# Value loops of a hybrid decoder block: unit words refilled by halves, first key quarters loaded early, second key input turned in other tiles

## The chip, the cores and the metric

The kernel runs on one core of a Trainium2 chip. The metric is device time in microseconds, the median of several runs. Engines are named as in the profile: PE (TensorE matmuls), PEld (its weight loads), DVE (VectorE), ACT (ScalarE), POOL (GpSimd), SP (SyncE, which here only issues DMAs).

## What is computed

One decoder block over 512 tokens of 2048 channels: RMSNorm, one wide input projection, two groups of attention heads side by side, each gated by a SiLU path, an output projection, a residual and a final RMSNorm. Cut to the parts near the change:

```python
h = _rmsnorm(x, norm_g[l])
proj = h @ w_in[l]
(qa, kca, vca, ksa, vsa, kwa, vwa, za, ga, qb, kb, vb, zb) = jnp.split(proj, offsets, axis=-1)
qa = _rope(_heads(qa, 8, 128))...
kc = _compress(_rope(_heads(kca, 2, 128)), cmp_k_pos[l], cmp_k_w1[l], cmp_k_w2[l])
vc = _compress(_heads(vca, 2, 128), cmp_v_pos[l], cmp_v_w1[l], cmp_v_w2[l])
o_cmp, p_cmp = _compressed_attention(qa, kc, vc)
o_sel = _selected_attention(qa, _rope(ksa), vsa, _select_blocks(p_cmp, S))
o_win = _banded_attention(qa, _rope(kwa), vwa, 512)
y_a = (gates . (o_cmp, o_sel, o_win)) * silu(za)
...
def _compress(kv, pos_emb, w1, w2):      # 31 blocks of 32 tokens, 16 apart, of each of 2 key heads
    flat = blocks of kv + pos_emb        # (B, 31, 2, 32 * 128)
    return silu(flat @ w1) @ w2          # w1: 4096 x 256
```

## The kernel before, in words

All matmuls work on fp32 inputs split into two words, hi (rounded, by ACT) and lo (the rest, by DVE: input minus hi); a product is three matmuls, L110 (hi by hi), L111 and L112 (hi by lo). A weight tile of 128x1024 (512 KB) is loaded by SP into one of the raw buffers (raw0, raw1, raw2, for keys and heads also raw3), split by ACT and DVE into the words whi and wlo (a pool of three buffers for each), and used by PE.

Three parts of the kernel matter here; they follow attention B, whose last part still runs beside the first rows below.

*Last projections and value loops.* Two projections kc, the compressed keys' inputs, lie in pj banks; `turned` (L769) applies the rope to each on DVE (products by L115 to L117 into t1 and t2, sum by L772) and writes kvt0. Then `proj(wz[18])` and `proj(wz[19])` (48 matmuls of 512 columns each) give the compressed values' inputs, which `values` (L763) scales into kvt1. Loop 1 runs over four chunks of the weights wv1: `tok_chunk` (48 matmuls of 256 columns) takes a chunk's words, and after each chunk two compress units of the keys (`compress_unit`, L653), each with two cw halves of 256 KB, split by L511/L512 into words, and 8 matmuls (L674, L675). `build(6)` and `build(7)` (L393 on) form words of x for the later products, also on ACT and DVE (L401 to L407). Loop 2 runs over eight chunks of wv0 (24 matmuls of 280 columns) with one compress unit of the values each. In loop 2, two loads for the keys are issued: a quarter at u = 3, and at u = 4 the sum of two quarters, the first loaded by SP, the second added on top by an accumulating DMA of POOL (`sums`, L739 to L741).

*Keys and heads.* Each of `keys(1)`, `keys(0)`, `pair(0)` (the first head's query and gate) and the later pairs runs `seven` (L538): seven products of 24 matmuls instead of eight, over four weight quarters x1, x2, x3, x4 (q3, q0, q1, q2 of the source) and sums of them. The products are named "22", "p", "21", "12", "u", "w", "q"; between them DVE and ACT form words and sums and run hooks. With `extra` a sum is formed by the DMAs: x4 gets q3 added by POOL (L567), and `extra()` returns the sum of q0 and q2 (for keys `fifth_sum`, for the first head `sum_of_head`, L830), which is split for "12". The key words of group 1 are written to DRAM by POOL in four transfers (`key_words`, L733, Kd<-k), those of group 0 go to KH and KL.

*Order.* Each engine does its instructions in its own order, which the scheduler of the framework sets from when the inputs and buffers come free; `tc.issue_after(x)` puts an instruction behind x in it. A DMA issued by SP or POOL waits for its buffer at the head of that engine's queue, with the later ones behind it.

Of the kernel before, what the change touches and what calls it, by code (L numbers as in the profile page):

```python
# [34 lines left out]
def hybrid_block(ctx, tc, xT, xtm, w0, wv0, wv1, wz, wq, wo0, wos, cw1, cw2, cpos, e2, rope, tabs, sinks, gT, fg, out):  # L35
# [430 lines left out]

    kvstack = xstack.enter_context(ExitStack())
    kv = kvstack.enter_context(sb("kvA", side="right"))
    KH = kv.tile([P, CMP + 1056], F32R, name="KH")[:, 0:CMP + 1024]
    KL = kv.tile([P, CMP + 1056], F32R, name="KL")[:, 0:CMP + 1024]  # L470
    VH, VL = [kv.tile([P, NQ - 1, 2, P], F32R, name=f"V{e}") for e in "HL"]
    VF = kv.tile([P, 2, 2, 256], F32, name="VF")
    VC = [kv.tile([P, P], F32R, name=f"VC{g}") for g in range(2)]
    pps = ExitStack()
    pp = pps.enter_context(sb("pp"))

# [173 lines left out]

        return qq, silu if h == 7 else silu()

    def compress_unit(b, u, acc):  # L653
        F = wk.tile([P, 4, P], F32R, name="F", tag=("ph", "pl")[u % 2])
        hi, lo = [F[:, :, e * 64:e * 64 + 64].rearrange("p j (g b) -> p j g b", g=2) for e in range(2)]
        off, j0 = u // 4, 4 * u % 16
        for g in range(2):
            src = kvts[b][:, g, j0:j0 + 4, off:off + 31]
            act.activation(hi[:, :, g, 0:31], src, AF.Copy)
            dve.tensor_tensor(out=lo[:, :, g, 0:31], in0=src, in1=hi[:, :, g, 0:31].bitcast(F32), op=ALU.subtract)  # L660
        for e, word in enumerate((hi, lo)):
            src = posw[:, b, 4 * u:4 * u + 4, e].unsqueeze(2).to_broadcast([P, 4, 2])
            dve.tensor_copy(word[:, :, :, 31], src)
        wh, wl = words(EVEN)
        for half in range(2):
            n = half if u % 2 else 2
            r = wk.tile([P, S], F32, name="cw", tag="st") if n == 2 else \
                wk.tile([P, S], F32, name="cw", tag=("qh", "ql")[n], bufs=1)
            last["dma"] = nc.sync.dma_start(r, cw1[:, b, u, half * S:half * S + S]).ins
            cs = slice(half * S, half * S + S)  # L670
            split(wh[:, cs], wl[:, cs], r)
        for j in range(4):
            cs = slice(j * 256, j * 256 + 256)
            pe.matmul(acc[:, 0:256], F[:, j], wh[:, cs], start=u == 0 and j == 0, stop=False)  # L674
            pe.matmul(acc[:, 0:256], F[:, j], wl[:, cs], start=False, stop=u == 7 and j == 3)  # L675
# [16 lines left out]
    def compressed_keys(acc):  # L692
# [3 lines left out]
            pe.matmul(kcp[:, 0:64], cw2s[:, 0, i, :], sl[:, i, :], start=i == 0, stop=i == 1)  # L696
        kct = pp.tile([P, 64], F32, name="kct")
        act.activation(kct, kcp[:, 0:64], AF.Copy, scale=0.5)
        k1 = pp.tile([P, 2, CMP], F32R, name="k1w")
        for g, (h, l) in enumerate(((KH[:, 0:CMP], KL[:, 0:CMP]), (k1[:, 0], k1[:, 1]))):  # L700
            src = kct[:, g * 32:g * 32 + 32]
            act.activation(h, src, AF.Copy)
            dve.tensor_tensor(out=l, in0=src, in1=h.bitcast(F32), op=ALU.subtract)
        for e in range(2):
            pool.dma_start(Kd[e, :, 0:CMP], k1[:, e].bitcast(F32))

    def compressed_values(sl):
        for g in range(2):
# [57 lines left out]
    def units(b, us):  # L766
        return [lambda u=u: compress_unit(b, u, cacc[b]) for u in us]

    def turned(ps, out):  # L769
        t1, t2 = rope_mul(wk.tile([P, S], F32, name="t1", tag="t1", bufs=1), wk.tile([P, S], F32, name="t2", tag="t2", bufs=1),  # L770
                          ps, cosA, sinA)
        dve.tensor_tensor(out=out, in0=by_block(t1), in1=by_block(t2), op=ALU.add)  # L772

    banks6 = [bank(e) for e in range(6)]
    vacc = [banks6[0:4], [banks6[4 + t // 2][:, t % 2 * 256:t % 2 * 256 + 256] for t in range(NQ)]]
    first_words = load_unit(wv1[:, 0], 1024, place=MOVING)
    for g in range(2):
        turned(kc[g], kvts[0][:, g, :, 0:32])
    for g in range(2):
        values(proj(wz[18 + g]), g)  # L780
    cacc = [psp.tile([P, S], F32, name="pj", tag="pj"), None]
    early, ready = [], []
    xr = rows(6)
    for u in range(4):
        tok_chunk(wv1, 4, 256, vacc[1], u, True, None if u else first_words)
        for n in (2 * u, 2 * u + 1):
            compress_unit(0, n, cacc[0])
        if u == 0:
            build(6, xr)
            xr = rows(7)  # L790
# [2 lines left out]
    for u in range(8):  # L793
# [4 lines left out]
            cacc[1] = bank(4)  # L798
        compress_unit(1, u, cacc[1])
        if u == 1:  # L800
            compressed_keys(csum)
        if u == 3:
            early.append(load_quarter(wq[0], tags[0], 3))
        if u == 4:
            ready.append(fifth(0))
            sums(*ready, wq[0], 0, 2)

    def gate_evac():
        for t in range(NQ):
# [3 lines left out]
        gc = gates[:, 0, :].rearrange("p (h b) -> p h b", b=3)[:, :, 0]  # L813
        dve.tensor_scalar(gc, gc, rowvalid, None, op0=ALU.mult)

    early += [load_quarter(wq[0], c, quarter) for c, quarter in zip(tags[1:], (0, 2, 1))]
    with tc.issue_after(last["lo"]):
        for ms in (slice(0, 4), slice(4, 8)):
            for e in range(2):
                pool.dma_start(even[e][:, ms], wd[e, :, ms])  # L820
            if not added:
# [607 lines left out]
```

## Time and profile before

| | |
|---|---|
| median of 3 runs | 816.33 us (812.87 to 817.54) |
| profiled execution | 813.13 us, span 811.4 us |
| PE busy | 794.7 us, 98% of the span |
| DVE busy | 689.7 us, 85% |
| ACT busy | 499.6 us, 62% |
| POOL busy | 91.9 us, 11% |
| DMA | 123.17 MB, mean 152 GB/s |

The span is the profiled execution from its first to its last instruction. Stages, by the trace: the two last projections and loop 1 from about 278 to 323 us, loop 2 to 357, keys(1) to 378, keys(0) to 399, pair(0) to 418, then the other heads, attention A and the output projection.

### The profile page before, as it was taken

The numbers are of one execution on the slowest core, as the hardware profiler recorded it, in microseconds if no ns is written. First come the engines' busy times: TensorE is split into PE (matmuls) and PEld (weight loads), VectorE is DVE, ScalarE is ACT, GpSimd is POOL, SyncE is SP. The second block draws the span as 40 slices with busy tenths as digits, with TensorE's granted clock in tenths as the row PEclk, the third lists the DMA queues.
The fourth block names the chain that finished last, engine by engine and source line by source line (L and its number), as shares of the span: only waits on it lengthen the run. The fifth ranks groups of instructions, "written<-read, shape, count | busy, mean of one in ns | idle before, by whom it ended". The sixth has DMA issues, their size and how long they took to land.

```text
span 811.4 us, 15259 instructions
## 1 busy us (share of the span) xinstructions
PE 794.7 (98%) x5690; PEld 741.5 (91%) x5690; DVE 689.7 (85%) x1410; ACT 499.6 (62%) x1092; POOL 91.9 (11%) x87
## 2 busy tenths in 40 slices
PE   9999999999999999999999999999999999999996
PEld 8787888888888889999999999999998989999996
DVE  7668989989897596668999999998998978877995
ACT  6646656555564456654447867877777857543545
POOL 3515000000010001232110111010000000000000
PEclk9999999999999999999999999999999999999999
DMA  7572242344343467888733214324335236697845
GB/s 237 168 241 80 78 142 82 114 130 156 98 149 92 151 184 219 277 249 213 194 88 105 78 40 118 104 73 152 103 140 174 81 103 244 218 240 204 254 89 208
DMA packets 46394, 123.17 MB, mean 152 GB/s; under 512 B 5520, under 2 KB 8368, under 8 KB 46320
## 3 DMA queue, kind: packets, MB, share of 16 engines
q1 hardware_dynamic: 42512, 109.32, 41.7%
q0 software_dynamic: 3520, 12.36, 7.5%
q8 instruction: 45, 0.74, 0.4%
q10 hardware_dynamic: 288, 0.52, 0.2%
q14 instruction: 29, 0.24, 0.1%
HBM read 110.08 MB, written 12.09 MB: 151 GB/s over the span
## 4 chain that ended last, share of the span: by engine, by line
PE 85%; DVE 6%; DMA 3%; issue 3%; ACT 2%; POOL 0%; SPq 0%; ACTq 0%; DVEq 0%; POOLq 0%
PE pj L110 16%; PE pj L112 16%; PE pj L111 16%; PE oa L111 5%; PE oa L110 5%; PE oa L112 5%; PE sp L870 4%; PE bank L112 2%; PE bank L111 2%; PE bank L110 2%; PE tp L369 2%; PE tp L905 1%; DMA raw<-wq 1%; DVE wlo L512 1%; DMA cw<-cw 1%
## 5 line engine op out<-in xcount | busy, mean ns | idle before, releaser
L110 PE MATMUL pj<-xh,whi 128*128 128x256 f32 (+1 forms) x592 | 197.2, 333 | 1.3 <-DVE kvt L764 1.1
L111 PE MATMUL pj<-xl,whi 128*128 128x256 f32 (+1 forms) x592 | 196.4, 332 | 0.0
L112 PE MATMUL pj<-xh,wlo 128*128 128x256 f32 (+1 forms) x592 | 196.3, 332 | 0.0
L110 PEld LDWEIGHTS pj<-xh,whi 128*128 128x128 f32 x592 | 111.4, 188 | 12.1 <-issue 1.5
L112 PEld LDWEIGHTS pj<-xh,wlo 128*128 128x128 f32 x592 | 111.4, 188 | 10.3 <-DVE wlo L512 0.2
L111 PEld LDWEIGHTS pj<-xl,whi 128*128 128x128 f32 x592 | 111.6, 188 | 9.6
L91 DVE TENSOR_TENSOR wlo<-raw,whi 128x1024 fp32r<-128x1024 f32 (+2 forms) x72 | 81.8, 1137 | 18.5 <-ACT whi L89 18.1
L512 DVE TENSOR_TENSOR wlo<-raw,whi 128x1024 fp32r<-128x1024 f32 x70 | 88.9, 1283 | 6.1 <-ACT whi L511 5.6
L511 ACT ACTIVATE whi<-raw 128x1024 fp32r<-128x1024 f32 x70 | 72.7, 1057 | 31.0 <-DVE raw L549 13.8
L89 ACT ACTIVATE whi<-raw 128x1024 fp32r<-128x1024 f32 (+2 forms) x71 | 65.1, 918 | 35.8 <-PE pj L111 20.9
L110 PE MATMUL oa<-whi,yh 128*128 128x256 f32 x200 | 55.6, 279 | 1.6 <-DVE sums L876 1.6
L111 PE MATMUL oa<-wlo,yh 128*128 128x256 f32 x200 | 55.6, 278 | 1.0 <-DVE wlo L973 1.0
L112 PE MATMUL oa<-whi,yl 128*128 128x256 f32 x200 | 55.4, 277 | 0.0
L110 PE MATMUL pj<-pu,whi 128*128 128x256 f32 x160 | 45.3, 283 | 0.2 <-DVE zr L549 0.2
L112 PE MATMUL pj<-pu,wlo 128*128 128x256 f32 x160 | 45.1, 282 | 0.3 <-DVE wlo L512 0.2
L111 PE MATMUL pj<-pu,whi 128*128 128x256 f32 x160 | 44.9, 280 | 0.0
L348 ACT ACTIVATE ttb<-ttb,sums 128x256 f32<-128x256 f32 (+1 forms) x64 | 30.0, 471 | 21.0 <-DVE sums L341 21.0
L273 ACT ACTIVATE ph<-tp 128x512 fp32r<-128x512 f32 (+1 forms) x64 | 34.1, 562 | 12.8 <-PE tp L905 7.7
L274 DVE TENSOR_TENSOR pl<-tp,ph 128x512 fp32r<-128x512 f32 (+1 forms) x64 | 40.4, 652 | 0.9 <-ACT ph L273 0.8
L110 PEld LDWEIGHTS oa<-whi,yh 128*128 128x128 f32 x200 | 37.5, 188 | 1.7 <-issue 1.7
L111 PEld LDWEIGHTS oa<-wlo,yh 128*128 128x128 f32 x200 | 37.6, 188 | 1.2 <-DVE wlo L973 1.2
L112 PEld LDWEIGHTS oa<-whi,yl 128*128 128x128 f32 x200 | 37.6, 188 | 0.0
(384 smaller groups left out, 2338.7 us busy)
## 6 DMA issues: line engine op xcount, KB each, us to landing
raw<-wq SPq DMA_DIRECT2D x43, 512.0 KB, 4.5
raw<-wz SPq DMA_DIRECT2D x36, 512.0 KB, 4.0
cw<-cw SPq DMA_DIRECT2D x32, 256.0 KB, 3.5
raw<-wos SPq DMA_DIRECT2D x14, 512.0 KB, 4.5
rw<-wos SPq DMA_DIRECT2D x10, 512.0 KB, 5.5
xr<-xT SPq DMA_DIRECT2D x16, 256.0 KB, 3.7
rows<-xT SPq DMA_DIRECT2D x8, 512.0 KB, 5.1
raw<-wo SPq DMA_DIRECT2D x8, 512.0 KB, 3.7
```

Source lines behind the costliest of these rows:

```text
L89: last["hi"] = act.activation(hi[:, :width], rw[:, :width], AF.Copy).ins
L91: last["lo"] = dve.tensor_tensor(out=lo[:, :width], in0=rw[:, :width], in1=hi[:, :width].bitcast(F32), op=ALU.subtract).ins
L110: pe.matmul(ps, ah, bh, start=first, stop=False, skip_group_check=go_on)
L111: pe.matmul(ps, ah, bl, start=False, stop=False, skip_group_check=go_on)
L112: recent["mm"] = pe.matmul(ps, al, bh, start=False, stop=last, skip_group_check=go_on).ins
L273: act.activation(ph, tp, AF.Copy)
L274: dve.tensor_tensor(out=pl, in0=tp, in1=ph.bitcast(F32), op=ALU.subtract)
L348: act.activation(tv, tv, AF.Exp, bias=mn[:, e, v:v + 1], scale=-1.0, accum_out=dn[:, e, v:v + 1])
L369: pe.transpose(tp[:, o:o + P], tts[kt + s][:, v, c0:c0 + P], ident)
L511: act.activation(hi, src, AF.Copy)
L512: last["lo"] = dve.tensor_tensor(out=lo, in0=src, in1=hi.bitcast(F32), op=ALU.subtract).ins
L870: pe.matmul(sp[:, a:b], qq[:, qs], kk[:, ko:ko + b - a], start=pi == 0, stop=pi == 2)
```

## The change

1. `turned` for the second group uses the tiles tagged qh and ql in place of t1 and t2. Before, the cw halves of unit 1 have these tags too.
2. Loop 1 has three standing pairs of word buffers (`places`). The compress units take `places[0]` and `places[1]` in turn; chunks 1 to 3 take `places[2]`, which is refilled in two halves of 512 columns, each with its own ACT and DVE instruction. Chunk 0 keeps its words from before.
3. KH and KL are not allocated until keys(1) is done. In their space stand two tiles, ahead0 and ahead1. Before loop 1, SP loads quarter 3 of the key weights into ahead0 and quarter 0 into ahead1, to which POOL adds quarter 2. Their loads in loop 2 are gone; at u = 3 a load of quarter 0 takes their place, in the buffer that was quarter 3's (tags[0]). The compressed keys' words of group 0 are kept in a small tile and copied into KH and KL by two ACT instructions behind keys(1).
4. `sum_of_head`'s load and accumulate are put behind the last DMA issued before it.

```diff
-    KH = kv.tile([P, CMP + 1056], F32R, name="KH")[:, 0:CMP + 1024]
-    KL = kv.tile([P, CMP + 1056], F32R, name="KL")[:, 0:CMP + 1024]
+    ahead = ExitStack()
+    quarters = [ahead.enter_context(sb(f"ahead{e}", side="right")).tile([P, 1024], F32, name=f"ahead{e}") for e in range(2)]
...
-    def compress_unit(b, u, acc):
+    def compress_unit(b, u, acc, pair=None):
...
-        wh, wl = words(EVEN)
+        wh, wl = pair or words(EVEN)
...
-    def turned(ps, out):
-        t1, t2 = rope_mul(wk.tile([P, S], F32, name="t1", tag="t1", bufs=1), wk.tile([P, S], F32, name="t2", tag="t2", bufs=1),
-                          ps, cosA, sinA)
+    def turned(ps, out, tags):
+        t1, t2 = rope_mul(*[wk.tile([P, S], F32, name="t", tag=tag, bufs=1) for tag in tags], ps, cosA, sinA)
...
-        turned(kc[g], kvts[0][:, g, :, 0:32])
+        turned(kc[g], kvts[0][:, g, :, 0:32], (("t1", "t2"), ("qh", "ql"))[g])
...
-    early, ready = [], []
     xr = rows(6)
+    early, ready = quarters[:1], quarters[1:]
+    with tc.issue_after(last["dma"]):
+        nc.sync.dma_start(*early, wq[0][3])
+        sums(*ready, wq[0], 0, 2)
+    places = [words(EVEN), words(EVEN), words(MOVING)]
+
+    def by_halves(src):
+        rw = raw()
+        last["dma"] = nc.sync.dma_start(rw, src).ins
+        for cs in (slice(0, 512), slice(512, 1024)):
+            split(places[2][0][:, cs], places[2][1][:, cs], rw[:, cs])
+        return places[2]
+
     for u in range(4):
-        tok_chunk(wv1, 4, 256, vacc[1], u, True, None if u else first_words)
+        tok_chunk(wv1, 4, 256, vacc[1], u, True, by_halves(wv1[:, u]) if u else first_words)
         for n in (2 * u, 2 * u + 1):
-            compress_unit(0, n, cacc[0])
+            compress_unit(0, n, cacc[0], places[n % 2])
...
-            early.append(load_quarter(wq[0], tags[0], 3))
-        if u == 4:
-            ready.append(fifth(0))
-            sums(*ready, wq[0], 0, 2)
+            with tc.issue_after(last["dma"]):
+                early.append(load_quarter(wq[0], tags[0], 0))
...
-    early += [load_quarter(wq[0], c, quarter) for c, quarter in zip(tags[1:], (0, 2, 1))]
+    early += [load_quarter(wq[0], c, quarter) for c, quarter in zip(tags[2:], (2, 1))]
...
+    ahead.close()
+    kv = kvstack.enter_context(sb("kvK", side="right"))
+    KH, KL = [kv.tile([P, CMP + 1056], F32R, name=f"K{e}")[:, 0:CMP + 1024] for e in "HL"]
+    for e, k in enumerate((KH, KL)):
+        act.activation(k[:, 0:CMP], k0w[:, e].bitcast(F32), AF.Copy)
     other = keys(0, {"22": [other]})
 
     def sum_of_head():
         t = fifth(0)
-        sums(t, wq[2], 0, 2)
+        with tc.issue_after(last["dma"]):
+            sums(t, wq[2], 0, 2)
         return t
```

The lines of the changed kernel are one higher from L467 on, two or three higher near L724, and about ten higher behind loop 1 (L567 is L568, L733 is L736, L741 is L744).

SP's queue just ahead of loop 1 (wv are value chunks, cw compress weights, yd attention results, wq key weights), before:

```order
L84 DMA raw<-wv 128x1024 x3
L257 DMA yd_83<-st 128x512
L499 DMA cw2s<-cw 128x512
L501 DMA E_2809<-e 128x64
L503 DMA pos<-cpos 128x64
L669 DMA cw<-cw 128x512 x5
L410 DMA wd<-wf 128x2x256
L390 DMA rows<-xT 128x1024
```

and after:

```order
L793 DMA raw<-wv 128x1024 x3
L257 DMA yd_83<-st 128x512
L500 DMA cw2s<-cw 128x512
L502 DMA E_2815<-e 128x64
L504 DMA pos<-cpos 128x64
L787 DMA ahead_2799<-wq 128x1024
L743 DMA ahead_2803<-wq 128x1024
L670 DMA cw<-cw 128x512 x7
L84 DMA raw<-wv 128x560
```

Two quarters stand in front of the cw halves, and more of these in one row.

DVE where the turned keys and scaled values are formed and build begins (kvt_2816 is kvt0, kvt_2817 kvt1), before:

```order
L772 TENSOR_TENSOR kvt_2816<-t_2832,t_2833 128x16x32
L764 TENSOR_TENSOR kvt_2817<-pj,rstdb 128x16x32
L115 TENSOR_TENSOR t_2838<-pj,cosA 128x512
L116 TENSOR_TENSOR t_2839<-pj,sinA 64x512
L117 TENSOR_TENSOR t_2839<-pj,sinA 64x512
L512 TENSOR_TENSOR wlo<-cw,whi 128x512
L660 TENSOR_TENSOR F<-kvt_2816,F 128x4x31 x4
L506 TENSOR_TENSOR posw<-pos,posw 128x64
L772 TENSOR_TENSOR kvt_2816<-t_2838,t_2839 128x16x32
```

and after (kvt_2822 is kvt0, kvt_2823 kvt1):

```order
L774 TENSOR_TENSOR kvt_2822<-t 128x16x32 x2
L767 TENSOR_TENSOR kvt_2823<-pj,rstdb 128x16x32
L513 TENSOR_TENSOR wlo<-cw,whi 128x512
L661 TENSOR_TENSOR F<-kvt_2822,F 128x4x31 x8
L507 TENSOR_TENSOR posw<-pos,posw 128x64
L664 COPY F<-posw 128x4x2 x8
L767 TENSOR_TENSOR kvt_2823<-pj,rstdb 128x16x32
L513 TENSOR_TENSOR wlo<-cw,whi 128x512 x3
L401 TENSOR_TENSOR rows<-rows 128x256
```

The second group's rope products (L115 to L117) are no longer between the two scaled values; they stand some fifteen rows higher. On PE, wz[19]'s 48 matmuls now stand ahead of chunk 0's, which before stood between wz[18] and wz[19].

POOL's queue through keys(0) to pair(0) (L567 and L741 accumulate a quarter, L733 writes key words; t is a later head's rope), before:

```order
L567 DMA raw<-wq 128x1024
L741 DMA raw_4454<-wq 128x1024
L733 DMA Kd<-k_4160 128x4x128
L733 DMA Kd<-k_4161 128x4x128
L733 DMA Kd<-k_4247 128x4x128
L733 DMA Kd<-k_4248 128x4x128
L567 DMA raw<-wq 128x1024
L630 TENSOR_TENSOR t_4438<-t_4438,t_4637 128x512
```

and after:

```order
L568 DMA raw<-wq 128x1024
L736 DMA Kd<-k_4155 128x4x128
L736 DMA Kd<-k_4156 128x4x128
L736 DMA Kd<-k_4251 128x4x128
L736 DMA Kd<-k_4252 128x4x128
L568 DMA raw<-wq 128x1024
L744 DMA raw_4458<-wq 128x1024
L631 TENSOR_TENSOR t_4442<-t_4442,t_4641 128x512
```

The head's accumulate moves from the second place to the seventh, behind x4's. Its load on SP likewise stands behind x4's load.

## Rows read from the trace of the kernel before

**Rows 1.** Busy time, share and instructions by engine, from the page.

```profile
PE 794.7 (98%) x5690; PEld 741.5 (91%) x5690; DVE 689.7 (85%) x1410; ACT 499.6 (62%) x1092; POOL 91.9 (11%) x87
```

**Rows 2.** Windows: length, busy us by engine (PE, PEld, DVE, ACT, POOL), PEclk, DMA share, GB/s.

```profile
275.00:278.00 3.00, 3.00 (x14) 2.46 (x14) 0.66 (x1) 0.00 (x0) 0.00 (x0) 1.00 0.91 294
278.00:330.00 52.00, 49.92 (x365) 46.36 (x364) 40.01 (x105) 30.98 (x76) 5.17 (x9) 1.00 0.65 196
376.00:412.00 36.00, 35.47 (x298) 34.93 (x298) 34.83 (x48) 15.73 (x22) 5.82 (x7) 1.00 0.73 180
416.00:460.00 44.00, 43.93 (x368) 43.28 (x367) 42.97 (x86) 31.13 (x75) 6.39 (x4) 1.00 0.21 66
```

**Rows 3.** Waits of PEld, 278 to 330: line, releaser, us in total, times, longest.

```profile
PEld pj L674 <- ACT whi L511: 0.8, 2, 0.6
PEld bank L111 <- DVE wlo L91: 0.6, 2, 0.3
PEld bank L674 <- ACT whi L511: 0.4, 1, 0.4
PEld bank L110 <- ACT whi L89: 0.4, 1, 0.4
```

**Rows 4.** Timeline of PE: start, us, operation [idle before, releaser]; wz[19] begins.

```profile
284.96 0.28 PE L112 MATMUL bank<-whi,xl 128*128 128x256 f32 x1
286.36 0.47 PE L110 MATMUL pj<-xh,whi 128*128 128x512 f32 x1 [1.12 <-DVE kvt L764]
```

**Rows 5.** Timeline of DVE, build(6): first and last of six rows.

```profile
293.96 0.45 DVE L401 TENSOR_TENSOR rows<-rows 128x256 f32<-128x256 f32 x1
...
296.09 0.42 DVE L404 TENSOR_TENSOR rows<-rows 128x256 f32<-128x256 f32 x1
```

**Rows 6.** Timeline of ACT: two splits of cw halves, loop 1 and 2.

```profile
289.00 0.63 ACT L511 ACTIVATE whi<-cw 128x512 fp32r<-128x512 f32 x1 [0.74 <-DMA cw<-cw]
...
326.13 0.63 ACT L511 ACTIVATE whi<-cw 128x512 fp32r<-128x512 f32 x1 [0.82 <-DMA cw<-cw]
```

**Rows 7.** Timeline of SP's queue: cw half 0b; x4 of pair(0).

```profile
286.17 0.33 SPq L669 DMA_DIRECT2D cw<-cw  x1
...
392.14 0.33 SPq L531 DMA_DIRECT2D raw<-wq  x1
```

**Rows 8.** DMAs issued from 316 to 322: KB each, median us to landing.

```profile
cw<-cw SPq DMA_DIRECT2D x4, 256.0 KB, 8.5
raw<-wq SPq DMA_DIRECT2D x1, 512.0 KB, 5.8
```

**Rows 9.** Timeline of POOL, keys(0) to pair(0).

```profile
382.88 0.89 POOL L741 DMA_DIRECT2D raw<-wq  x1 [6.01 <-DVE wlo L512]
385.06 0.80 POOL L733 DMA_DIRECT2D Kd<-k  x1 [1.28 <-issue]
389.58 0.79 POOL L733 DMA_DIRECT2D Kd<-k  x1 [3.72 <-DVE zr L549]
...
399.04 0.75 POOL L733 DMA_DIRECT2D Kd<-k  x1 [4.93 <-DVE t L627]
399.78 0.97 POOL L567 DMA_DIRECT2D raw<-wq  x1
```

**Rows 10.** DMAs of POOL, issued 375 to 412, then L741's alone (382 to 384).

```profile
raw<-wq POOLq DMA_DIRECT2D x3, 512.0 KB, 7.8
Kd<-k POOLq DMA_DIRECT2D x4, 256.0 KB, 3.8
...
raw<-wq POOLq DMA_DIRECT2D x1, 512.0 KB, 5.5
```

**Rows 11.** Timeline of DVE, then PE, in pair(0): the sum's words; product "u".

```profile
403.98 1.23 DVE L512 TENSOR_TENSOR wlo<-raw,whi 128x1024 fp32r<-128x1024 f32 x1
...
409.43 2.36 DVE L512 TENSOR_TENSOR wlo<-raw,whi 128x1024 fp32r<-128x1024 f32 x2 [0.52 <-ACT whi L511]
...
410.69 0.28 PE L110 MATMUL pj<-pu,whi 128*128 128x256 f32 x1
```

More of the change, by code (lines that the diff above doesn't have):

```diff
@@ L473, in hybrid_block @@
     VC = [kv.tile([P, P], F32R, name=f"VC{g}") for g in range(2)]
+    ahead = ExitStack()
+    quarters = [ahead.enter_context(sb(f"ahead{e}", side="right")).tile([P, 1024], F32, name=f"ahead{e}") for e in range(2)]
+    KH = KL = None
     pps = ExitStack()
@@ L698, in compressed_keys @@
         act.activation(kct, kcp[:, 0:64], AF.Copy, scale=0.5)
-        k1 = pp.tile([P, 2, CMP], F32R, name="k1w")
-        for g, (h, l) in enumerate(((KH[:, 0:CMP], KL[:, 0:CMP]), (k1[:, 0], k1[:, 1]))):
+        k0, k1 = [pp.tile([P, 2, CMP], F32R, name=f"k{g}w") for g in range(2)]
+        for g, (h, l) in enumerate(((k0[:, 0], k0[:, 1]), (k1[:, 0], k1[:, 1]))):
             src = kct[:, g * 32:g * 32 + 32]
@@ L705, in compressed_keys @@
             pool.dma_start(Kd[e, :, 0:CMP], k1[:, e].bitcast(F32))
+        return k0
     def compressed_values(sl):
@@ L723, in key_words @@
     def key_words(v, g, w):
-        views = [k[:, CMP:].rearrange("p (t w c) -> p w t c", w=2, c=P)[:, w] for k in (KH, KL)]
-        if g:
+        if not g:
+            views = [k[:, CMP:].rearrange("p (t w c) -> p w t c", w=2, c=P)[:, w] for k in (KH, KL)]
+        else:
             tiles = [wk.tile([P, S], F32R, name="k1", tag="ph"), wk.tile([P, S], F32R, name="k1", tag="pl")]
@@ L800, in hybrid_block @@
         if u == 1:
-            compressed_keys(csum)
+            k0w = compressed_keys(csum)
         if u == 3:
-            early.append(load_quarter(wq[0], tags[0], 3))
-        if u == 4:
-            ready.append(fifth(0))
-            sums(*ready, wq[0], 0, 2)
+            with tc.issue_after(last["dma"]):
+                early.append(load_quarter(wq[0], tags[0], 0))
     def gate_evac():
```

## The prediction

> **What bounds the kernel now.** I read the page first: PE is busy 98% of the span [rows 1], so an edit can win only idle time of PE, or lose by making some. So I looked for PE's idle time stage by stage. In the windows [rows 2] the stage 278 to 330, which holds the last two projections and the first value loop, has PE busy for 49.92 of 52 us; the stage of the keys and the first head, 376 to 412, for 35.47 of 36; 416 to 460 for 43.93 of 44. PE's granted clock is 1.00 in all of them, its upper level of 2.4 GHz, so no term comes from the clock. DVE is the near second: 34.83 of 36 us and 42.97 of 44. Time that DVE loses there can't be made up. Next I asked what PE's idle 2.1 us of 278 to 330 wait for. The waits of the weight loads [rows 3] name words of compress units (L674 on ACT L511), the value words of a whole chunk (L111 on DVE L91) and, after it, a chunk whose ACT part is late (L110 on ACT L89); the timeline of PE [rows 4] names one more, the largest, at the start of proj(wz[19]): from 284.96 to 286.36 it waits for DVE's L764, which frees the pj bank. Last I read the queues on which the change puts transfers, SP's [rows 7] and POOL's [rows 9], with what their transfers took [rows 8, 10], and the consumers of the head's sum [rows 11].
>
> **The change part by part.** Sizes: a quarter is 512 KB, a half unit of compress weights (cw) 256 KB.
>
> *Turned keys in other tiles.* Kernel before: the second group's rope products share t1/t2 with the first, stand behind it on DVE, and hold the pj bank that proj(wz[19]) wants. In the new order DVE forms them before the last projections end, and PE does wz[18], wz[19], then chunk 0. The 1.12 us wait and what follows it go: 286.36 - 284.96 less one spacing of 0.11 is **-1.3 us**. Next late there would be the words of wz[19], which have been waiting for a free bank only. Bounds 0 (something else holds the bank) and -1.3.
>
> *Words by halves.* A chunk's 1024-column split (1.06 us ACT, 1.22 us DVE at L91) becomes two of half the length; matmuls begin when the first half is there. Halves cost about 0.1 us more per engine, which ACT (31 of 52 us busy) and DVE (40 of 52) hide [rows 2]. The three standing pairs let a compress unit be filled while the one before is read. Against this part stand 0.8 (L674 pj) and 0.6 (L111) [rows 3], so 1.4 at most. The first refill still waits for all of chunk 0, whose buffer it takes, so I leave a third: **-1.0 us**, bounds 0 and -1.4.
>
> *Quarters out of the loop.* Before, one quarter and a sum (two quarters, the second an accumulate by POOL) are issued at 311 to 318. Beside them the four cw issued between 316 and 322 take a median 8.5 us to land [rows 8], and 326.13 starts after 0.82 us of waiting for its cw [rows 6]. With those 1.57 MB gone only a single later quarter shares with cw. The two waits that follow are 0.4 + 0.4 (bank L674, bank L110) [rows 3]: **-0.6 us**, bounds 0 and -0.8.
>
> *The same quarters at the front.* They go out on SP just ahead of cw 0b, 1a and 1b, which were issued from 286.17 on [rows 7], 0b being converted at 289.00 [rows 6]. Two plain quarters (1.05 MB) at the 294 GB/s of three such loads, 275 to 278 [rows 2], take 3.6 us: 0b at 292.6, 1a and 1b, 0.26 MB each, 0.9 apart to 294.4. PE needs units 0 and 1 at 296.0 (286.36 plus 48 matmuls of 0.23, less the 1.3) and chunk 1 at 297.9 (16 of 0.12 later). What decides is DVE, in order: 1b's lo, then six operations of build (from L401 at 293.96 to the end of L404 at 296.51: 2.5 us [rows 5]), then chunk 1's first half. After 1b's landing that is 0.6 for ACT, 0.65 for its lo, 2.5, and 0.3 until the half serves: 4.0, so 1b must be there by 293.9. **+0.5 us**, bounds 0 and the rival below. The transfers don't share only with SP's: the accumulate on POOL follows the landing of its first quarter, and the 8.5 us of [rows 8] were taken with such an accumulate in flight. The Trainium skill's page "DMA: Bandwidth & Descriptors", section "Issuing engines are not separate DMA queues", says the same as a rule: DMAs of all issuing engines run on the same 16 DMA engines and interleave, so moving a load to another issuer saves only issue time. By it the accumulate's bytes would have to be counted in front of 1b as well, as in the slower rival; with plain quarters alone the term is 0.5.
>
> *raw0 free earlier.* The first key product's quarters q3 and q0 of keys(0) can load some microseconds earlier. PE idles 0.53 us in all from 376 to 412 [rows 2]: **-0.3 us**, bounds 0 and -0.5. The compressed keys' two copies into KH and KL (ACT, 128x32) lie in a stage where ACT is busy 15.73 of 36 us: nothing; without that cover, some 0.4.
>
> *The head's sum behind its x4.* This one speaks against the change. Before, POOL accumulates the first head's sum at 382.88 (L741), ahead of the four Kd writes; and DVE forms its lo words at 403.98 [rows 9, 11]. Now the load stands behind pair(0)'s x4 on SP (392.14 [rows 7]; with the 5.8 us of a quarter in [rows 8] in by 398), and the accumulate behind four Kd writes and x4's own accumulate. In [rows 9] the Kd writes start a landing apart (385.06, 389.58, ..., the last 399.04; median 3.8 to land [rows 10]), while 399.78 follows 399.04 at once: POOL's queue seems to take one Kd write and one accumulate together, not another on top. Without L741 ahead the first can go 1.28 us sooner, at 383.8, and the last three landings later, at 395.2; or it stays at 399.04. x4's accumulate follows at once, the sum's when that Kd write has landed: from 399.0 to 402.8. I take 399.6, near the early end, since nothing else is left in that queue to hold the first write. An accumulate took 7.8 us (median of three), L741 5.5 [rows 10]. So the sum is in at 407.4; ends 404.5 (399.0 + 5.5) and 410.6. DVE's L512 at 403.98, behind ACT's split of 1.06, needs it by 402.9 to be undisturbed, so DVE, in order, stands 4.5 us. Its rows follow one another without a gap up to the 0.52 us in front of 409.43, and PE's product "u" at 410.69 needs that row's first half with 0.3 to spare: 0.84 us is taken up. **+3.7 us** (ends +0.8 and +6.9). Behind it PE and DVE are both full from 416 to 460 [rows 2], so it stays.
>
> *Sum.* -1.3 - 1.0 - 0.6 + 0.5 - 0.3 + 3.7 = **+1.0 us**. The profiled execution took 813.13 us, 3.2 under the median of 816.33; against itself 814.1, against the median 817.3. With all bounds -4.0 + 0.8 to +6.9 + 0.5 - 1.3, some 813.1 to 822.4.
>
> **The rivals.**
> *The sum comes in time (faster side).* If POOL's queue has more room than I read, the Kd writes go out as their data come, and the accumulate can start with its load's landing, by 398, and with 5.5 us be in at 403.5: a stall under the 0.84. For it: L741's 5.5; against it: the spacing of the Kd writes in [rows 9]. Then the gains stay: -1.3 - 1.0 - 0.6 - 0.3 = -3.2, 813.1; with all bounds at their ends 812.3.
>
> *The early quarters starve the first units (slower side).* Decided by 1b's landing after 293.9. Had the 1.57 MB, accumulate included, and the three cw (0.79 MB) to drain before it at the 180 GB/s of 376 to 412 [rows 2], a stretch with three accumulates, it would land 13.1 us after 286.2, at 299.3: 5.4 us late instead of 0.5. With the rest of the sum: +5.9, 822.2. For it: the 8.5 us of [rows 8]; against it: the issue order puts cw right behind the two plain quarters, and the accumulate can start only when its quarter is in.
>
> *The halves bring nothing.* If a refill's first matmul still waits for both halves, or for the buffer, the 1.0 goes: +2.0, 818.3. For it: the first refill's wait for chunk 0; against it: chunks 2 and 3 have none.
>
> **How the numbers follow.** Forecast 0.47, sum in time 0.25, starved units 0.15, halves idle 0.13. A measurement of this kernel tells about 0.5% (4.1 us) from no change: 812.2 to 820.4. The forecast lies within it but for its upper end (0.42 same, 0.04 slower, 0.01 faster); the sum in time lies at its lower edge and is given 0.18 faster, 0.07 same; starved units 0.11 slower, 0.04 same; idle halves 0.11 same, 0.02 slower. Together faster 0.19, same 0.64, slower 0.17. The time is the forecast's, 817.3. The range takes in the first rival's lower end, less about 1 us since the three runs shown lie 4.7 us apart and a median of such may move so far, and the second rival's time: 811.3 to 822.2.
>
> **What would show each step.** In the trace after: proj(wz[19]) begins without a gap behind wz[18], else the first term is wrong. The waits of L674 and the value matmuls from 278 to 330 add to under 1 us, else the halves or early quarters are. The cw after the early quarters land in under 4 us. The wait that decides is at the first head: an idle DVE ahead of L513 for the head's sum, some 4.5 us, and PE idle at the product "u" for about 3.7. If DVE runs there without a gap, the last term falls and the time is near 813. If the accumulate lands past 410, it is nearer 820. A new wait after 416 would make the whole sum wrong.

## The result: slower, by a late sum and by a wait that the prediction had not seen

The changed kernel takes 822.13 us (median of 12 runs, 817.32 to 824.76), the kernel before 815.7 (12 runs, 812.87 to 818.35). The ratio on record is 1.0064, with a 95% interval of 1.0044 to 1.0084; it is an estimate over the runs and not the quotient of the two medians, which is 1.0079. The forecast was 817.3; the measured time lies 0.07 us inside the upper end of the range (822.2), on the slower side of 0.5%, which had a chance of 0.17. The profiled execution took 817.57 us with a span of 815.8, against 813.13 and 811.4 before: both are near the low end of their runs, and their difference, 4.4 us, is what the traces have to explain. The medians differ by 6.4 us; the other 2 have no trace. In nine of the eleven other runs of the changed kernel the mean granted clock was lower (0.990 to 0.994) than in the profiled one (0.995).

The rows of after that answer to [rows 2] (windows: length, then busy us and instructions of PE, PEld, DVE, ACT, POOL, then PEclk, DMA share, GB/s):

```profile
278.00:330.00 52.00, 50.58 (x374) 47.88 (x373) 39.69 (x109) 31.38 (x82) 5.25 (x9) 1.00 0.71 216
376.00:412.00 36.00, 30.70 (x254) 29.99 (x253) 30.02 (x41) 13.28 (x18) 4.87 (x6) 0.99 0.61 160
416.00:460.00 44.00, 43.61 (x371) 42.95 (x370) 42.53 (x81) 29.63 (x68) 6.38 (x4) 1.00 0.22 72
```

PE's idle time up to 330 us fell from 2.1 to 1.4 us, and from 376 to 412 it rose from 0.5 to 5.3. What PE waits for in the whole trace of after, the two waits that are new (releaser, us in total, times, longest):

```profile
PE pj L110 <- DVE t L550: 4.6, 2, 4.4
...
PE bank L110 <- ACT whi L89: 1.3, 1, 1.3
```

The first is the head's sum: PE waits for a DVE result that stands in DVE's order behind the sum's words. POOL's timeline of after answers to [rows 9] (start, us, operation, in brackets the idle time before it and its releaser), and ACT's, DVE's and PE's in pair(0) to [rows 11]; the last block is DVE's row of before that frees the bank of PE's product "12":

```profile
382.11 0.78 POOL L736 DMA_DIRECT2D Kd<-k  x1 [7.39 <-ACT k L732]
...
394.13 0.76 POOL L736 DMA_DIRECT2D Kd<-k  x1 [3.98 <-DVE wlo L513]
395.05 0.92 POOL L568 DMA_DIRECT2D raw<-wq  x1 [0.16 <-issue]
398.69 0.89 POOL L744 DMA_DIRECT2D raw<-wq  x1 [2.73 <-issue]
```

```profile
406.23 1.06 ACT L512 ACTIVATE whi<-raw 128x1024 fp32r<-128x1024 f32 x1 [5.63 <-DMA raw<-wq]
...
407.32 1.23 DVE L513 TENSOR_TENSOR wlo<-raw,whi 128x1024 fp32r<-128x1024 f32 x1 [5.25 <-ACT whi L512]
...
410.22 0.36 PE L110 MATMUL pj<-xh,whi 128*128 128x256 f32 x1 [4.40 <-DVE t L550]
```

```profile
406.32 0.42 DVE L549 TENSOR_TENSOR t<-t,pj 128x256 f32<-128x256 f32 x1
```

The last key write goes at 394.13 and takes 4.3 us to land; the sum's accumulate (L744) goes at 398.69, 0.26 us behind that landing, though its own load had landed at 396.3, and it is in 7.5 us later. ACT waits for it until 406.23, DVE stands for 5.25 us, PE for 4.56 us beyond its spacing. The second wait is told with the runs. The early quarters did what the forecast said: PE has no wait between 278 and 320 but a gap of 0.34 us at chunk 1, 0.22 more than its spacing.

### The profile page after: what moved, and what is told of

It reads as the page before. It is cut to its first block, busy times and chain, and to the rows that moved or that the text cites. A ratio compares the mean times of both kernels' runs of the same rounds, so it can differ in the third digit from the quotient of the medians.

```text
span 815.8 us, 15273 instructions
## 1 busy us (share of the span) xinstructions
PE 793.9 (97%) x5690; PEld 741.7 (91%) x5690; DVE 690.5 (85%) x1413; ACT 500.4 (61%) x1097; POOL 93.1 (11%) x87
## 4 chain that ended last, share of the span: by engine, by line
PE 74%; DVE 10%; DMA 7%; ACT 4%; issue 3%; SPq 0%; POOL 0%; DVEq 0%; ACTq 0%; POOLq 0%
PE pj L110 14%; PE pj L112 14%; PE pj L111 14%; PE oa L111 4%; PE oa L112 4%; PE oa L110 4%; PE sp L888 3%; DMA raw<-wq 3%; DVE wlo L513 2%; DMA cw<-cw 2%; PE bank L112 2%; PE bank L110 2%; PE bank L111 2%; PE tp L369 1%; PE tp L923 1%
## 5 line engine op out<-in xcount | busy, mean ns | idle before, releaser
L110 PE MATMUL pj<-xh,whi 128*128 128x256 f32 (+1 forms) x592 | 197.7, 334 | 5.0 <-DVE t L550 4.6
L111 PE MATMUL pj<-xl,whi 128*128 128x256 f32 (+1 forms) x592 | 196.9, 333 | 0.0
L110 PEld LDWEIGHTS pj<-xh,whi 128*128 128x128 f32 x592 | 112.1, 189 | 15.8 <-issue 5.0
L111 PEld LDWEIGHTS pj<-xl,whi 128*128 128x128 f32 x592 | 112.2, 189 | 9.6
L91 DVE TENSOR_TENSOR wlo<-raw,whi 128x1024 fp32r<-128x1024 f32 (+2 forms) x69 | 79.1, 1147 | 21.1 <-ACT whi L89 20.6
L513 DVE TENSOR_TENSOR wlo<-raw,whi 128x1024 fp32r<-128x1024 f32 (+1 forms) x72 | 86.7, 1217 | 10.0 <-ACT whi L512 9.6
L512 ACT ACTIVATE whi<-raw 128x1024 fp32r<-128x1024 f32 (+1 forms) x72 | 72.3, 1020 | 36.4 <-DVE raw L550 13.9
L89 ACT ACTIVATE whi<-raw 128x1024 fp32r<-128x1024 f32 (+2 forms) x68 | 61.9, 913 | 36.6 <-PE pj L111 25.2
L110 PE MATMUL oa<-whi,yh 128*128 128x256 f32 x200 | 55.4, 278 | 1.6 <-DVE sums L894 1.6
L111 PE MATMUL oa<-wlo,yh 128*128 128x256 f32 x200 | 55.7, 279 | 1.0 <-DVE wlo L991 1.0
L110 PE MATMUL pj<-pu,whi 128*128 128x256 f32 x160 | 45.2, 282 | 0.4 <-DVE zr L550 0.4
L111 PE MATMUL pj<-pu,whi 128*128 128x256 f32 x160 | 44.7, 279 | 0.0
L110 PEld LDWEIGHTS oa<-whi,yh 128*128 128x128 f32 x200 | 37.5, 188 | 1.7 <-issue 1.7
L111 PEld LDWEIGHTS oa<-wlo,yh 128*128 128x128 f32 x200 | 37.6, 188 | 1.2 <-DVE wlo L991 1.2
```

The source lines that it names most:

```text
L89: last["hi"] = act.activation(hi[:, :width], rw[:, :width], AF.Copy).ins
L91: last["lo"] = dve.tensor_tensor(out=lo[:, :width], in0=rw[:, :width], in1=hi[:, :width].bitcast(F32), op=ALU.subtract).ins
L110: pe.matmul(ps, ah, bh, start=first, stop=False, skip_group_check=go_on)
L111: pe.matmul(ps, ah, bl, start=False, stop=False, skip_group_check=go_on)
L512: act.activation(hi, src, AF.Copy)
L513: last["lo"] = dve.tensor_tensor(out=lo, in0=src, in1=hi.bitcast(F32), op=ALU.subtract).ins
```

## The experiments

All were run beside the kernel before (medians 814.85 to 815.56). For each the text on record comes first. The traces are compared by the start of one ACT row in each, which exists in all kernels: the first value evacuation behind loop 1 (L482 of the kernel before), and the copy behind product "22" (L576) in keys(1), in pair(0), in the next pair, and in the one at 481 us. Rows of the kernel before: 320.55, 361.51, 402.41, 425.04, 481.45. The table gives each kernel's start less that of before, in us (negative is sooner), and the span less 811.4. Each row of it is one profiled execution. The spans of sum_as_before, sum_unbound, late_sum_filled and turned_alone also hold the wider spacing of matmuls told of at the end, so spans are not to be compared from row to row. The rows of loop 1 and keys(1) are ACT's and can lag behind PE: by PE's first matmul of keys(1), 356.83 before, the changed kernel is 1.53 us ahead, sum_as_before 0.47, value_tiles_swapped 3.97, turned_alone 2.32 and halves_alone 1.38, and quarters_alone is 0.23 behind.

| kernel | loop 1 | keys(1) | pair(0) | next pair | at 481 | span | ratio on record (95%) |
|---|---|---|---|---|---|---|---|
| changed | -0.55 | -2.00 | -2.20 | +3.75 | +3.49 | +4.4 | 1.0064 (1.0044 to 1.0084) |
| sum_as_before | -1.00 | -0.53 | -0.79 | -0.97 | -1.25 | +4.2 | 1.0011 (0.9987 to 1.0035) |
| late_sum_alone | +0.48 | +1.14 | +0.95 | +8.29 | +8.03 | +8.0 | 1.0085 (1.0054 to 1.0115) |
| sum_unbound | +2.29 | +3.36 | +3.47 | +3.47 | +3.48 | +8.8 | 1.0037 (1.0013 to 1.0061) |
| late_sum_filled | -1.56 | -3.34 | -3.49 | +3.07 | other order | +12.1 | 1.0126 (1.009 to 1.0163) |
| value_tiles_swapped | -3.14 | -4.77 | -5.31 | -5.49 | -5.76 | -2.8 | 0.9954 (0.9926 to 0.9982) |
| turned_alone | -1.41 | -3.13 | -2.33 | -2.33 | -2.59 | +8.4 | 1.0064 (1.0042 to 1.0085) |
| halves_alone | -1.35 | -2.10 | -1.92 | -2.11 | -2.39 | -1.0 | 0.998 (0.9955 to 1.0006) |
| quarters_alone | +1.12 | -0.50 | -0.72 | -0.72 | -0.72 | +1.1 | 0.9993 (0.9969 to 1.0016) |
| sum_before_x4_on_pool | -0.63 | -0.45 | -1.03 | +4.79 | +4.80 | +4.7 | 1.004 (1.0018 to 1.0061) |
| changed_tiles_swapped | -2.30 | -3.82 | -3.87 | +3.64 | +3.37 | +4.1 | 1.0049 (1.0026 to 1.0072) |

### Taking the late sum away, and adding it alone

sum_as_before, on the changed kernel (`mark` is keys(0)'s last quarter load):

```diff
+        last["mark"] = last["dma"]          # in seven, behind x3's load
...
-        with tc.issue_after(last["dma"]):
+        with tc.issue_after(last["mark"]):
             sums(t, wq[2], 0, 2)
```

> The changed kernel, with the head's sum back near its old place: its load behind the last key load of keys(0), its accumulate ahead of the four key writes. Theory (late sum): all of the loss comes from that place, 4.6 us of idle PE and 1.6 us at half clock behind it; without it the time is 6.2 us under the changed kernel, about 2 us under before, ratio 0.997, and the granted clock stays at 1.00 from 400 to 430. Rival (front part): the early quarters or the new wait ahead of loop 2 cost what was lost; then the ratio stays at 1.004 to 1.006.

late_sum_alone, on the kernel before:

```diff
-        sums(t, wq[2], 0, 2)
+        with tc.issue_after(last["dma"]):
+            sums(t, wq[2], 0, 2)
```

> The kernel before, with one edit: the head's sum (load and accumulate) behind the last DMA, as in the changed kernel. Theory (late sum): 5.5 to 6.5 us over before, ratio 1.007 to 1.008, with DVE idle for about 5 us ahead of the sum's lo words and PE for about 4.5. Rival (front part): ratio 1.000 to 1.002.

Measured: 815.45 us without it in the changed kernel, 6.7 under 822.13, and 822.23 with it alone, 6.7 over its kernel before (815.56). In the table the column "next pair" less "pair(0)" is what the head loses: 5.95 us changed, 7.34 alone, and -0.18 without the late sum. So the sum's place is shown to cost time from both sides. The size is less sure: by the ratios on record it is 0.53% and 0.85%, 4.3 and 6.9 us, and each interval in them is 0.4% to 0.6% wide. What was not as expected in sum_as_before: without it the kernel should have been 2 us faster than before, and is level with it (1.0011). The gain that the changed kernel had at pair(0), 2.2 us, was only 0.8 here.

sum_unbound takes the `issue_after` away altogether:

> The changed kernel without the order on the head's sum: the scheduler then issues its load and accumulate in loop 1, among the cw loads, where the kernel before had the key sum. Theory (late sum): no stall at the head; the cw loads behind it come late again, 0.4 to 1.0 us of PE in loop 2, so 1.0 to 1.6 us under before, ratio 0.998 to 0.999. Rival (front part): ratio 1.005.

The head indeed loses nothing (+3.47 and +3.47), but the theory's 0.4 to 1.0 us in loop 2 were 4.3, in one wait, and the ratio was 1.0037 where 0.998 to 0.999 was expected. That wait was the one that had been 1.3 us in the changed kernel, and it led to the next runs.

### The wait ahead of loop 2

In the changed kernel PE stands ahead of the first matmul of loop 2, since ACT is late with its words. ACT's timeline, then PE's, of the changed kernel; then ACT's of sum_unbound, and ACT's of the kernel before:

```profile
320.00 0.47 ACT L483 ACTIVATE vt<-bank,small 128x256 f32<-128x256 f32 x1 [3.11 <-DMA wd<-wf]
...
321.13 0.67 ACT L89 ACTIVATE whi<-raw 128x560 fp32r<-128x560 f32 x1
...
321.85 0.39 PE L110 MATMUL bank<-whi,xh 128*128 128x280 f32 x1 [1.35 <-ACT whi L89]
```

```profile
322.84 0.47 ACT L483 ACTIVATE vt<-bank,small 128x256 f32<-128x256 f32 x1 [5.47 <-DMA wd<-wf]
```

```profile
320.55 0.48 ACT L482 ACTIVATE vt<-bank,small 128x256 f32<-128x256 f32 x1 [3.00 <-PE bank L112]
```

ACT's first evacuation behind loop 1 writes a tile tagged t1, and t1 still holds wf, the words of build(7), until their store to DRAM has landed. Before, the same row waited for PE. The store does not come sooner than before, though loop 1 does. SP's timeline of the changed kernel, then of the kernel before:

```profile
286.92 8.60 SPq L670 DMA_DIRECT2D cw<-cw  x7
298.82 0.33 SPq L84 DMA_DIRECT2D raw<-wv  x1
299.91 2.88 SPq L670 DMA_DIRECT2D cw<-cw  x3
302.85 0.42 SPq L410 DMA_DIRECT2D wd<-wf  x1
303.32 0.46 SPq L390 DMA_DIRECT2D rows<-xT  x1
...
316.07 0.38 SPq L410 DMA_DIRECT2D wd<-wf  x1
```

```profile
297.45 0.38 SPq L410 DMA_DIRECT2D wd<-wf  x1
297.88 0.46 SPq L390 DMA_DIRECT2D rows<-xT  x1
...
316.04 0.43 SPq L410 DMA_DIRECT2D wd<-wf  x1
```

The rows of x that build(7) needs (L390) are loaded at 303.32, behind ten cw halves instead of five; before it was 297.88. They have one buffer (tag raw3) with the rows of build(6), whose last words ACT formed at 296.55 before and forms at 301.53 now, in order behind the split of a cw half for which it waits until 300.08:

```profile
300.08 0.63 ACT L512 ACTIVATE whi<-cw 128x512 fp32r<-128x512 f32 x1 [1.90 <-DMA cw<-cw]
...
301.53 0.40 ACT L406 ACTIVATE wf<-rows 128x256 fp32r<-128x256 f32 x1
```

So the later load goes back to the later cw halves. ACT waits 1.7 us for the rows, and the store goes at 316.07 (316.04 before) and takes 3.8 us. Whether it would have gone sooner with the rows in time was not run. value_tiles_swapped is sum_as_before with one edit that takes the tile away from the store:

```diff
-... tag=(("qh", "ql"), ("t1", "pcr"))[w][t // 2], bufs=1)
+... tag=(("qh", "ql"), ("pcr", "t1"))[w][t // 2], bufs=1)
```

> As sum_as_before, and in the evacuation behind loop 1 the first value tile takes the buffer pcr and the third takes t1, which build(7)'s words hold until their store to DRAM has landed. Theory (store): the 1.4 to 1.6 us that PE waits ahead of loop 2 are ACT standing behind that store, so they go, and with them what the clock loses there: 1.5 to 2 us under sum_as_before, ratio 0.998. Rival (buffers): the first words of loop 2 wait for one of the three standing pairs, and the wait stays, ratio 1.001.

Measured: 810.3 us, a ratio of 0.9954 (0.9926 to 0.9982), the fastest of all. ACT's row now waits for PE, and the windows hold no idle time of PE:

```profile
317.41 0.47 ACT L483 ACTIVATE vt<-bank,small 128x256 f32<-128x256 f32 x1 [1.12 <-PE bank L112]
```

```profile
300.00:320.00 20.00, 20.00 (x174) 20.00 (x173) 15.73 (x46) 14.76 (x37) 0.87 (x2) 1.00 0.72 232
320.00:330.00 10.00, 10.00 (x82) 10.00 (x81) 8.04 (x23) 7.89 (x24) 3.40 (x6) 1.00 0.85 260
```

The theory of the store holds and the rival of the buffers falls; the size was 4.6 us (0.57%, the difference of the two ratios, with intervals of some 0.25% to either side), not 1.5 to 2. Part of it is the clock. In sum_as_before PE stood idle for 1.76 us at 321.39, and in the windows behind it:

```profile
320.00:322.00 2.00, 0.61 (x4) 0.56 (x4) 0.63 (x1) 2.00 (x8) 0.86 (x2) 1.00 0.51 187
322.00:324.00 2.00, 1.99 (x12) 1.81 (x11) 1.27 (x5) 2.00 (x9) 0.88 (x2) 0.74 0.38 102
324.00:326.00 2.00, 2.00 (x11) 2.00 (x10) 2.00 (x5) 1.51 (x6) 1.83 (x4) 0.50 0.63 198
326.00:328.00 2.00, 2.00 (x17) 2.00 (x17) 0.83 (x5) 1.40 (x3) 0.67 (x1) 0.91 0.93 270
```

Granted clock 0.74, 0.50 and 0.91 of full speed (the lower level, 1.2 GHz, for some 3.4 us) take 0.52 + 1.0 + 0.18 = 1.7 us. In the changed kernel's profile the wait at the same place (1.52 us idle at 321.85) was followed by a clock of 1.00; that is most of why it kept 2.0 us at keys(1) and sum_as_before only 0.5.

### The parts one by one

turned_alone is the kernel before with the new `turned`, halves_alone with `places` and `by_halves`; quarters_alone is the changed kernel with the old `turned`, the old words and the head's sum as in sum_as_before.

> The kernel before with the second key input turned in qh and ql alone. Theory: wz[19] follows wz[18] without a gap, chunk 0 comes behind it, 1.3 us are gained by 300 us and kept to the heads; nothing is lost there; ratio 0.998 to 0.9985. Rival (given back): the next wait of loop 1 takes it, 0 to 0.3 us left at the keys, ratio 1.000.

> The kernel before with the three standing pairs and the refill by halves alone. Theory: the waits for words inside loop 1 (1.4 us) fall to 0.3, so 1.0 us are gained at the end of loop 1. Theory (store): a wait of 1 us or more ahead of loop 2 appears here too, because loop 1 ends earlier and the store of build(7) does not. Rival: it appears only where the quarters are loaded early. Ratio 0.999 to 1.000.

> The early key quarters alone: t1 and t2 for both key inputs, words as before, the head's sum near its old place. Theory: the cw loads of loop 2 come without waiting (0.6 us gained in 324 to 328), cw 0b to 1b come up to 5 us later but in time (0 to 0.5 us lost by 300); ratio 0.999 to 1.000. Rival (starved units): more than 1 us lost by 305, ratio over 1.001.

At 481 us they gain 2.59, 2.39 and 0.72 us: together 5.70, and value_tiles_swapped, which has all three and neither of the two waits, gains 5.76. So in these traces, one of each kernel, the parts add, and each was worth more than forecast (1.3, 1.0 and 0.4). The ratios of halves_alone and quarters_alone are not clear of 1. Up to the end of loop 1 the first two agree with the forecast (-1.41 and -1.35); the rest comes behind it. There the waits for cw of 0.39 and 0.45 us (326.82 and 327.38 before) are gone in turned_alone, and 0.62 is left in halves_alone; by PE's first matmul of keys(1) turned_alone gains 0.91 us over loop 1, which is those two waits, and the rest of its 3.13 at keys(1) is ACT's own order. In quarters_alone loop 1 ends 1.12 us later than before, 0.5 of it in the stages before wz[19], and 0.4 more at chunk 1, where PE idles for 0.71 us; the rival of starved units asked for over 1 us lost by 305 and a ratio over 1.001. At 305 the loss is 1.11 us (ACT's value split that PE releases, 306.52 against 305.41), but 0.53 of it lies ahead of the units, and the ratio is 0.9993: the rival is not borne out, though the quarters lost more than the 0 to 0.5 us of the theory. No wait ahead of loop 2 appears in halves_alone (store at 315.37) or in quarters_alone (loop 1 ends late): as far as these two runs tell, it takes both, an earlier loop and a store that does not come earlier with it.

turned_alone is slower in all, 1.0064, though it is 2.6 us ahead at 481. Its loss, some 11 us, lies behind 652. The scheduler has put the matmuls of its output projection in another order, with PE waits of 3.5 and 1.7 us there (oa L111 on DVE's wlo L972, oa L110 on ACT's L971) and a granted clock of 0.54 from 695 to 700; that is some 7 us, and the last 4 are the wider spacing told of at the end. So it is argued, not shown, that this order and not the turn costs it; the new turn with the old order behind it is what value_tiles_swapped has, but for two matmuls.

### The place on POOL, and the clock behind the wait

sum_before_x4_on_pool lets POOL issue the head's accumulate ahead of x4's, still behind the four key writes, its load left late on SP:

> The changed kernel with one edit: POOL issues the head's accumulate ahead of x4's accumulate, behind the four key writes as before; the load on SP stays where the change put it. Theory (room in POOL's queue): the accumulate no longer stands behind x4's, goes when its load has landed (396.3) and not when the last key write has (398.4), lands about 2 us sooner, and since DVE sets the pace behind the wait the time falls by as much: 1.5 to 2.5 us under the changed kernel, ratio 1.0035 to 1.0045. Rival (the load's place on SP decides): nothing changes, ratio 1.0064.

```profile
396.37 0.76 POOL L737 DMA_DIRECT2D Kd<-k  x1 [4.67 <-DVE wlo L513]
398.67 0.92 POOL L745 DMA_DIRECT2D raw<-wq  x1 [1.54 <-DMA raw<-wq]
400.68 0.89 POOL L569 DMA_DIRECT2D raw<-wq  x1 [1.09 <-issue]
```

```profile
407.17 1.23 DVE L513 TENSOR_TENSOR wlo<-raw,whi 128x1024 fp32r<-128x1024 f32 x1 [3.10 <-ACT whi L512]
```

The accumulate goes as its load lands, beside the key write in flight; now x4's (L569) has to wait, until 400.68, and the key write of 396.37 landed 4.1 us after its issue, at 400.5. In the changed kernel and in the three other profiles with the old order on POOL, too, the second accumulate goes 0.2 to 0.3 us behind the landing of the last key write. So in all five POOL's queue holds one key write and one accumulate and not another, as the forecast read it. DVE's wait falls from 5.25 to 3.10 us and the time to 818.08, a ratio of 1.004, as expected, though its interval and that of the changed kernel overlap. The place on POOL is 2.1 of the 5.25 us; the rest is put down to the load's late place on SP, since the accumulate now goes as that load lands. In this profile the head still loses 5.8 us (-1.03 to +4.79), as the clock takes more behind the wait than in the changed kernel: 2.8 against 1.7 us, told of below.

late_sum_filled puts matmuls into PE's wait in the changed kernel (their result is read by nobody):

```diff
...
+        with tc.issue_after(recent["mm"]):
+            for k in range(36):
+                last["fill"] = pe.matmul(fb[:, 0:256], xh[:, k % KT, 0:P], xh[:, k % KT, 0:256], start=True, stop=True).ins
...
```

> The changed kernel with 36 matmuls of 256 columns, whose result nobody reads, on PE between products 21 and 12 of pair(0), where PE waits for the late sum: 36 times 0.118 is 4.25 us of the 4.56 us of idle time. Theory (the idle time lowers the clock): with PE at work the granted clock stays at 1.00 behind the wait, and the time falls by 1.6 us against the changed kernel, to a ratio of 1.0044. Rival (the clock's fall costs nothing, because DVE sets the pace behind the wait): the ratio stays at 1.006.

The clock stayed at 1.00, yet from the start of product "12" to the next pair's "22" copy it took 18.79 us, against 18.57 in the changed kernel and 17.18 in the kernel before. The run can't decide it: the scheduler moved ACT's copy behind "12" past a split, PE waited 1.10 us for it, and the order of the later heads changed too: behind 600 PE has waits that the changed kernel's trace lacks (2.8 us at 656.75, 1.4 at 631.97), which with the wider spacing make most of the 12.1 us of its span. The run changed_tiles_swapped bears on the same question: the changed kernel, late sum and all, with the two value tiles swapped.

> The changed kernel with the first and third value tile behind loop 1 swapped (pcr and t1), the head's sum left late. Theory: the two costs add, so what the swap gave beside sum_as_before (4.6 us, 0.57%) it gives here too, or the 2.8 us that the traces of the changed kernel and value_tiles_swapped show between loop 1 and the keys: ratio 1.001 to 1.003, with the 5 us wait of DVE ahead of the head's sum unchanged. Rival (the late sum swallows what comes in front of it, because its landing is set by transfers and not by PE): ratio 1.005 to 1.0065.

It comes to pair(0) 1.67 us sooner than the changed kernel and leaves it 0.11 sooner; in all 1.0049, between what the two theories gave. DVE's wait is 5.64 us, and the sum is in 1.2 us sooner, so 0.4 us go there. The rest is in the clock. Windows behind the wait, changed kernel first, changed_tiles_swapped second:

```profile
408.00:410.00 2.00, 0.00 (x0) 0.00 (x0) 2.00 (x5) 0.07 (x1) 0.00 (x0) 1.00 0.00 0
410.00:412.00 2.00, 1.78 (x11) 1.81 (x12) 2.00 (x4) 0.69 (x1) 0.00 (x0) 0.76 0.03 8
412.00:414.00 2.00, 2.00 (x12) 2.00 (x11) 1.75 (x3) 1.83 (x3) 0.00 (x0) 0.50 0.69 236
414.00:416.00 2.00, 2.00 (x17) 2.00 (x17) 2.00 (x3) 0.40 (x2) 0.00 (x0) 0.89 0.24 47
```

```profile
408.00:410.00 2.00, 1.02 (x5) 1.05 (x6) 2.00 (x4) 0.00 (x0) 0.00 (x0) 0.50 0.04 8
410.00:412.00 2.00, 2.00 (x11) 2.00 (x11) 1.75 (x3) 1.93 (x3) 0.00 (x0) 0.50 0.48 115
412.00:414.00 2.00, 2.00 (x11) 2.00 (x11) 2.00 (x3) 0.59 (x2) 0.00 (x0) 0.50 0.38 147
414.00:416.00 2.00, 2.00 (x16) 2.00 (x15) 1.59 (x3) 1.34 (x2) 0.00 (x0) 0.79 0.74 190
```

From the start of "12" (410.22 and 408.98) the clock takes 0.48 + 1.0 + 0.22 = 1.7 us in the one and 0.5 + 1.0 + 1.0 + 0.4 = 2.9 in the other; the same windows of sum_before_x4_on_pool give 2.8. From "12" to the next "22" these three take 18.57, 19.70 and 19.75 us. Less the clock that is 16.9, 16.8 and 16.9: what differs among them is the clock. The first 1.7 us are not all on the path, though: without any loss it is 17.18 before. So the clock's price in the changed kernel is about 1.4 us (18.57 less 17.18); that is an estimate, since the run meant to show it directly did not.

## Why the prediction came out as it did

Its direction held (+1.0 forecast, slower measured) and its leading mechanism was shown, but it was right by misses of opposite sign, and that the time lies in the range is luck. The range's upper end, 822.2, was the time of the rival of starved units, which did not occur; it was counted from a base of 816.33, and from the later 815.7 it would be 821.6, under the 822.13 measured. The sum "with all bounds" also keeps the turn's -1.3 in its upper end, where that term's bound is 0.

- *Turned keys, -1.3; halves, -1.0; quarters, -0.6, -0.3 and +0.5.* The mechanisms were right: the wait of [rows 4] is gone, no fill inside loop 1 waits for more than 0.34 us, cw 1b was in time. A half costs each engine more than the 0.1 us assumed (0.63 twice against 1.06 on ACT), and that stayed hidden. The terms were too small, 2.7 in all against 5.7 shown. They were taken as the sum of the waits in one window of before, and the halves' as two thirds of those; with all three edits every wait up to 330 us goes, those of loop 2 too. That makes 3.97 us by PE's first matmul of keys(1); the last 1.8 come in the keys and heads and were not followed to single waits.
- *The step that is missing.* Nothing was said of ACT ahead of loop 2. "Next late there would be the words of wz[19]" looked one step on and not at the end of the loop. The diff showed that two more cw and two quarters come ahead on SP; the load of build(7)'s rows stands behind them, and its words in the buffer that the first evacuation wants. In the changed kernel's profile it takes up to 2.8 us (2.00 us ahead at keys(1), where value_tiles_swapped is 4.77; 2.0 by PE's first matmul of loop 2, 321.85 against 319.81), and between sum_as_before and value_tiles_swapped 4.6 us by the ratios.
- *The head's sum, +3.7.* The queue was read rightly: the accumulate went at 398.69 and was in at 406.2. Counted from pair(0)'s own shift of 2.2 us that is 408.4 on the clock of before, against 407.4 forecast. The place was read wrongly, in "0.84 us is taken up" with product "u" as the first to suffer: PE stopped one product sooner, at "12", whose bank is freed by DVE's L550 (L549 at 406.32 before), which stands behind the sum's lo words in DVE's order. That cost the size little, as 0.69 us was taken up (5.25 less 4.56). The term's main miss is the clock, which it put at nothing, since PEclk was 1.00 in every row of before: behind the wait of 4.56 us PE ran at half clock for some 3.4 us. In all the head lost 5.95 us, 2.2 more than the 3.7: some 1.4 by the clock, 0.75 by DVE's longer wait (5.25 for 4.5).
- *The rivals.* The sum in time was not what happened; starved units neither. On the second, the rule of the Trainium skill's page "DMA: Bandwidth & Descriptors", section "Issuing engines are not separate DMA queues", agrees with one pair of rows: in sum_unbound SP's store of build(7) goes at 316.53 beside POOL's accumulate (314.51, 7.1 us to landing) and takes 6.2 us, where in the changed kernel, without that accumulate, it took 3.8. At the early place the accumulate did no harm that the traces show.
- *The checks it named.* wz[19] without a gap and DVE idle for some 4.5 us ahead of the head's sum (5.25): seen. Waits under 1 us from 278 to 330: PE's idle time there was 1.4 us, nearly all of it the wait ahead of loop 2, so this check failed, though not by the halves or the quarters alone, to which it was tied. PE idle at "u": it was at "12". "The cw after the early quarters land in under 4 us" was wrong (median 5.8 for seven). It cost the units nothing, but the half for which ACT waits until 300.08, ahead of the late rows of build(7), is one of them.
- *Net.* At 481 us: -5.8 for the parts, +2.8 for the store, +0.5 that value_tiles_swapped gains behind keys(1) and the changed kernel does not, +6.0 for the head, +3.5. The last 0.9 us of the span's 4.4 come in the output stage, at 662 to 701 us, where PE has a wait of 0.67 us at 695.22 that the kernel before has not; why stays open.

## What to carry to other kernels

When a loop is made faster, follow every buffer that the code behind it takes, back to the DMA that frees it: a store whose own input was loaded later than before can be next, and here that cost 2 to 4.6 us. A transfer is late by the slowest of its queues, so for each one that is moved look at what stands ahead of it on every issuer and at who is in order behind its reader; the price is the reader's whole standstill where nothing behind it has slack, and the clock's fall behind that. And judge an order that a scheduler makes by all of the trace: an edit at 280 us won 2.6 us, and its kernel lost some 7 behind 660, where the order had changed.

## What the runs showed of the hardware

PE's clock fell after a wait in some executions and not in others with the same wait. A gap of 1.73 us ahead of the output projection was followed by a granted clock of 1.00 in the kernel before (654.74) and by 0.66 over 5 us in sum_as_before (653.45). Ahead of loop 2, PE idle for 1.52 us at 321.85 (changed kernel) ran on at 1.00; idle for 1.76 at 321.39 (sum_as_before), it fell to 0.50 and lost 1.7 us. Behind gaps of 4.56 and 5.20 us it fell both times, in one case 0.9 us after PE was at work again, in the other while it stood. So in these traces an idle microsecond of PE cost up to about two. The mean granted clock does not sort the 35 executions of the unchanged kernel, which span 810.2 to 819.9 us: those at 0.995 alone lie from 811.5 to 819.9.

In the last 100 us matmuls of 256 columns came 4% further apart in some executions (427 instead of 444 in the 50 us from 720, PE busy throughout and the granted clock at 1.00): sum_as_before lost some 4 us there against before in that way. What sets it was not found.
